# Reordering one layer's attention stage: half a gate ahead of an up projection, an earlier start of NSA attention, and another order of building operands

## The chip, the cores and the metric

The kernel runs on one core of a Trainium2 chip. The metric is the device time of one execution in microseconds (us); smaller is better. Five engines run side by side, each with its own queue worked off in order: PE (TensorE, matrix products), DVE (VectorE), ACT (ScalarE), POOL (GpSimd) and SP (which only issues transfers here). An instruction that waits holds up all that is queued behind it on its engine.

## The reference

One decoder layer on 256 tokens with a model width of 2048, in float32:

```python
xn = _rms(x, norm_attn[l])
(fq, fk, fv, f_logit, nq, kc, vc, ksl, vsl, kw, vw,
 nsa_gate, gate_a, gate_b) = jnp.split(xn @ w_in[l], points, axis=-1)
...
o_a = _fox_attention(fq, fk, fv, log_f)
...
merged = (jax.nn.sigmoid(gate_a) * (o_a @ w_up_fox[l])
          + jax.nn.sigmoid(gate_b) * (o_b @ w_up_nsa[l]))
x = x + (merged @ w_out[l]).astype(x.dtype)
hn = _rms(x, norm_ffn[l])
x = x + ((jax.nn.silu(hn @ w_ffn_gate[l]) * (hn @ w_ffn_up[l])) @ w_ffn_down[l]).astype(x.dtype)
```

FoX attention has 8 heads of 128 with a forget decay. NSA attention has 8 heads of 192 in two groups, and each head adds three softmaxes (compressed, selected, window), each with its own gate. The 2048 columns of `sigmoid(gate_a)` multiply the FoX up projection column by column.

## The kernel before

Every float32 matrix is split into a rounded part `hi` and a rest `lo`, and a product is made of three matmuls: hi·hi, hi·lo, lo·hi. ACT makes `hi` of a weight tile (L171), DVE makes `lo` (L172). The tokens stand in two tiles of 128 rows (`t` = 0, 1).

The program is one long list, `stream`, which a loop at the end walks. Its first part, up to the index `ffn`, consists of *chunks*: 256 rows of a weight, 512 columns at most, 12 matmuls (L194 to L196) into the two `acc` banks of a projection (four banks in all, so that two projections can hold banks at once). The chunks are the input projection, then `w_up_fox`, then two projections of 512 columns each for the first half of `gate_a` (`ga_chunk`). A chunk's weights are loaded up to 8 chunks ahead and split up to 3 ahead (`SPLIT_AHEAD`).

From `ffn` on come *pairs*: 256 rows and 1024 columns of a weight. A plain pair has 24 matmuls. A *seven* has 21: it works on sums of operand blocks in the way of Strassen, and its weights are split in two parts. The first unit of eight pairs makes the second half of `gate_a`. A pair's 1 MB of raw weights is loaded by SP (L1092) into three tiles in turn, the third of which lies in the pool `ypool`; its `hi`, `lo` lie in one of four part buffers. A *thin* pair takes half of its `lo` by a DMA that adds the weights onto −hi (L1114, L1115).

Beside the stream run *tasks*, Python generators: after every chunk one slot, after every pair two slots, and in a slot up to two tasks emit their next step. `yield n` means that the next step comes n slots later. This sets where a task's instructions stand in each engine's queue. The tasks that matter here:

- `head_norm` and its callers make the normed queries and keys out of `acc` banks; the NSA queries come in four tasks (`st["nq"]`), one for each two heads. The last read of the banks is L354, L356.
- `fox_attention`: 10 steps. Step s makes the output of head s−2, the transposes of head s−1 (L711), the scores of head s (L722, L723) and its softmax (`softmax_parts`: DVE maximum L678, ACT exponential L680). `divide` (L683 to L689) is the DVE work that ends a softmax; the transposes need it.
- `nsa_attention`: the same for 10 steps, with transposes L774 to L780, scores L801 to L805, outputs L760 to L764. It first waits, slot by slot, until the tasks that it needs and the FoX task are over.
- `x_seven`: makes the operand of a seven for two k blocks of x (seven blocks of 128 columns, 7·128·2 floats a partition), four steps: DVE L1237, ACT L1238; DVE L1241, L1244, L1245 and ACT L1243; ACT L1247; DVE L1249. `x_sevens` makes the four in turn, begun nine chunks before `ffn`.

`up_a_evac` copies the FoX up projection to the tiles `ga` (L893 on ACT, L894 on DVE); `ga_chunk` later makes the sigmoid into a scratch tile (L908 on ACT) and multiplies it on (L910 on DVE).

Of the kernel before, what the change touches and what calls it, by code (L numbers as in the profile page):

```python
# [14 lines left out]
P = 128  # L15
# [39 lines left out]
def hybrid_block(ctx: ExitStack, tc: tile.TileContext, x, norm_attn, w_in, fox_f_bias,  # L55
# [80 lines left out]
    def spawn(gen):  # L136
        tk = Task(gen)
        tasks.append(tk)
        return tk
# [556 lines left out]
    def fox_attention():  # L696
# [3 lines left out]
        for s in range(FH + 2):  # L700
# [14 lines left out]
            if h < FH:  # L715
# [10 lines left out]
                                        (sc[:, 0:P], bf[:, 0:P], pb[h][:, 0:P])], None)  # L726
                yield 1
                divide()
                yield 2
            else:  # L730
                yield 3


    def nsa_attention():
        for tk in st["nq"][:1] + [st["gate"], st["cmp", 0], st["cmp", 1], st["fox"]]:
            while not tk.over:
                yield 1
        qa, qb = st["nqa"], st["nqb"]
# [9 lines left out]
        for s in range(NH + 2):  # L748
            if 0 < s <= NH:
                divide()  # L750
            h = s - 2
            if h >= 0:
# [35 lines left out]
            if h < NH:  # L788
# [7 lines left out]
                for c0, n, t in ((0, 272, 1), (272, 256, 1), (P, 272, 0)):  # L796
# [16 lines left out]
                                        (sc[0][:, 256:271], bf[:, 527:542], p[:, 784:799])], gsw[:, h])  # L813
            yield 1 if 5 < s else 2

# [16 lines left out]
    def nq_evac(h0, c0):  # L832
        def done(accs):
            if "nqa" not in st:
                st["nqa"] = u8(ypool, [P, NH, T])
                st["nqb"] = u8(ypool, [P, NH, T], F32R)
            if c0:
                st["decay"] = spawn(fox_decay([accs[t][:, 0:8] for t in range(NT)]))
            st.setdefault("nq", []).append(spawn(nsa_qk(
                accs, c0, 2, DK ** -0.5, lambda t, a, b: put_q(h0, a, b, t))))  # L840
            if h0 == 2:
                st["nsa"] = spawn(nsa_attention())
        return done
# [3 lines left out]
    def proj(c0, n, done, **kw):  # L847
        return gemm(w_in, c0, n, KB, sx, done, **kw)
# [38 lines left out]

    def up_a_evac(i):
        def done(accs):
            if i == 0:  # L890
                ga.extend(u8(mpool, [P, D]) for _ in range(NT))
            sl = slice(i * 512, (i + 1) * 512)
            nc.scalar.activation(ga[0][:, sl], accs[0], AF.Copy)  # L893
            nc.vector.tensor_copy(ga[1][:, sl], accs[1])  # L894
        return done
# [4 lines left out]
    for i in range(4):  # L900
        stream += gemm(w_up_fox, i * 512, 512, 8, stat_o("oTf"), up_a_evac(i))


    def ga_chunk(i):
        def done(accs):
            for t in range(NT):
                g = wk([P, 512], "qs", 4)
                nc.scalar.activation(g, accs[t], AF.Sigmoid, scale=rx[:, t:t + 1])  # L908
                sl = ga[t][:, i * 512:(i + 1) * 512]
                nc.vector.tensor_tensor(sl, sl, g, op=ALU.mult)  # L910
        return done

    for i in range(2):
        stream += proj(OFF_GA + 512 * i, 512, ga_chunk(i))

# [315 lines left out]
    def x_seven(kp, pool):  # L1231
# [13 lines left out]
        nc.vector.tensor_tensor(fo[:, 3], ao[:, 2], fo[:, 2], op=ALU.add)  # L1245
        yield 1
        nc.scalar.activation(d[:, 0, 3:7].rearrange("p o t -> p (o t)"), f, AF.Copy)  # L1247
# [8 lines left out]
    def x_sevens():  # L1256
        for kp in range(4):
            yield from x_seven(kp, ypool if kp < 3 else xpool)
            yield 1

    def put_m(kp, where):
# [6 lines left out]
    SX = (0, 1, 2, 3)  # L1268
    unit((4, 5, 0, 6, 1, 3, 2, 7), SX[:3], two(w_in, 0, OFF_GA + 1024), x_pair(SX[:3]), ga_evac(1), thin=(6, 7))
    for i in range(2):  # L1270
# [136 lines left out]
    def run_att(i, ch):  # L1407
        nonlocal nload
        if i == ffn - 9:
            open2()  # L1410
            spawn(x_sevens())
        while nload < min(i + LOAD_AHEAD, ffn):
# [114 lines left out]
```

## Time and profile before

| | |
|---|---|
| time, median of 3 runs | 1429.4 us (1429.39 to 1431.14) |
| the profiled execution's own time | 1432.12 us |
| its span, first to last instruction | 1430.4 us |
| PE busy | 1413.9 us, 99% of the span |
| DVE, ACT, POOL busy | 1189.7, 845.5, 119.0 us |
| granted TensorE clock, mean | 0.997 of full |

PE is the engine that all others serve. Its busy time counts a matmul from start to a modelled end, and matmuls overlap; so the time between two starts, not a matmul's own length, tells how fast PE goes: some 0.23 us for 512 columns and 0.17 us for 384. A row of a timeline that ends in brackets tells that the engine was idle before it, for how long, and what ended the wait. The clock that PE is granted has two levels, 1.2 and 2.4 GHz, shown as 0.5 and 1.0 of full.

### The profile page before, as it was taken

What the parts mean: (1) busy time and instruction counts of PE and PEld (TensorE: products, weight loads), DVE (VectorE), ACT (ScalarE), POOL (GpSimd) and SP (SyncE); (2) the same over time, 40 slices, a digit from 0 to 9 for tenths busy, and PEclk for the clock granted to TensorE, in tenths of its full rate; (3) what the DMA queues carried; (4) which work ended last, traced back from release to release, by engine and by line L of the source; (5) the groups of instructions that cost most, each with busy time, mean ns of one, the idle gap of its engine ahead of it and who ended that gap; (6) DMA issues with size and microseconds to landing.
All of it is one profiled execution on the core that took longest, in us unless ns stands there. A gap on an engine that the chain in (4) does not pass through costs nothing.

```text
span 1430.4 us, 18345 instructions
## 1 busy us (share of the span) xinstructions
PE 1413.9 (99%) x6692; PEld 1188.3 (83%) x6692; DVE 1189.7 (83%) x1536; ACT 845.5 (59%) x1075; POOL 119.0 (8%) x123
## 2 busy tenths in 40 slices
PE   9999999999999999999999999999999999999998
PEld 7888888998888878888888888888888888888887
DVE  6676866776776798779898999988999988899985
ACT  5566554456665566465566667556667645666742
POOL 0211010000000010010020001011101000110000
PEclk9999999999999999999999999999999999999999
DMA  7667876454346588786786787679888677988785
GB/s 273 199 220 209 258 244 181 132 154 137 119 136 202 162 242 265 227 235 173 255 239 206 222 271 214 234 219 251 246 238 243 222 212 235 247 247 241 219 240 159
DMA packets 167350, 308.58 MB, mean 216 GB/s; under 512 B 10286, under 2 KB 33420, under 8 KB 167132
## 3 DMA queue, kind: packets, MB, share of 16 engines
q1 hardware_dynamic: 150396, 273.77, 58.4%
q0 software_dynamic: 16688, 33.37, 13.5%
q8 instruction: 52, 0.85, 0.2%
q14 instruction: 38, 0.31, 0.1%
q10 hardware_dynamic: 176, 0.27, 0.1%
HBM read 298.98 MB, written 8.40 MB: 215 GB/s over the span
## 4 chain that ended last, share of the span: by engine, by line
PE 88%; DVE 3%; issue 3%; DMA 3%; ACT 2%; POOL 0%; SPq 0%; POOLq 0%; DVEq 0%; ACTq 0%
PE m L1144 15%; PE m L1145 14%; PE m L1143 14%; PE acc L194 8%; PE acc L196 8%; PE acc L195 8%; PE acc L1143 5%; PE acc L1145 5%; PE acc L1144 5%; DMA lo<-in_w_ffn_up_dram 1%; DVE lo L172 1%; PE acc L1060 1%; PE m L559 1%; PE m L560 1%; ACT hi L171 1%
## 5 line engine op out<-in xcount | busy, mean ns | idle before, releaser
L1121 DVE TENSOR_TENSOR lo<-raw,hi 128x2048 fp32r<-128x2048 f32 (+2 forms) x168 | 305.9, 1823 | 33.9 <-ACT hi L1119 16.9
L1119 ACT ACTIVATE hi<-raw 128x1536 fp32r<-128x1536 f32 (+1 forms) x129 | 217.3, 1687 | 107.3 <-PE m L1145 53.6
L172 DVE TENSOR_TENSOR lo<-raw,hi 128x1024 fp32r<-128x1024 f32 (+5 forms) x165 | 189.4, 1152 | 92.9 <-ACT hi L171 88.3
L1112 ACT ACTIVATE hi<-sums 128x1024 fp32r<-128x1024 f32 x148 | 154.5, 1059 | 140.2 <-PE m L1145 63.9
L194 PE MATMUL acc<-hi,u 128*128 128x512 f32 (+4 forms) x576 | 223.2, 388 | 2.5 <-ACT u L893 1.2
L196 PE MATMUL acc<-hi,u 128*128 128x512 f32 (+4 forms) x576 | 217.7, 378 | 0.0
L195 PE MATMUL acc<-lo,u 128*128 128x512 f32 (+4 forms) x576 | 217.4, 377 | 0.0
L171 ACT ACTIVATE hi<-raw 128x1024 fp32r<-128x1024 f32 (+5 forms) x165 | 161.9, 1001 | 68.6 <-PE acc L196 49.7
L1121 DVE TENSOR_TENSOR lo<-sums,hi 128x2048 fp32r<-128x2048 f32 x74 | 169.1, 2285 | 7.3 <-ACT hi L1112 7.0
L1144 PE MATMUL m<-lo,u 128*128 128x512 f32 x352 | 137.4, 390 | 2.1 <-DVE lo L1121 1.7
L1144 PE MATMUL m<-lo,hp 128*128 128x512 f32 x352 | 137.2, 390 | 1.4 <-DMA lo<-in_w_ffn_up_dram 1.4
L1143 PE MATMUL m<-hi,hp 128*128 128x512 f32 x352 | 137.9, 392 | 0.0
L1143 PE MATMUL m<-hi,u 128*128 128x512 f32 x352 | 137.4, 390 | 0.0
L1145 PE MATMUL m<-hi,hp 128*128 128x512 f32 x352 | 137.1, 389 | 0.0
L1145 PE MATMUL m<-hi,u 128*128 128x512 f32 x352 | 137.0, 389 | 0.0
L194 PEld LDWEIGHTS acc<-hi,u 128*128 128x128 f32 x576 | 108.9, 189 | 19.5 <-ACT u L893 1.7
L196 PEld LDWEIGHTS acc<-hi,u 128*128 128x128 f32 x576 | 108.7, 189 | 17.7 <-DVE u L277 0.7
L195 PEld LDWEIGHTS acc<-lo,u 128*128 128x128 f32 x576 | 108.9, 189 | 15.0
L1102 DVE TENSOR_TENSOR sums<-raw 128x1024 f32<-128x1024 f32 x68 | 82.9, 1219 | 1.0 <-DMA raw<-in_w_ffn_down_dram 0.7
L1144 PEld LDWEIGHTS m<-lo,u 128*128 128x128 f32 x352 | 66.1, 188 | 17.1 <-DVE lo L1121 2.3
L1144 PEld LDWEIGHTS m<-lo,hp 128*128 128x128 f32 x352 | 66.1, 188 | 15.7 <-DMA lo<-in_w_ffn_up_dram 2.4
L1145 PEld LDWEIGHTS m<-hi,hp 128*128 128x128 f32 x352 | 66.1, 188 | 13.7
(334 smaller groups left out, 2649.4 us busy)
## 6 DMA issues: line engine op xcount, KB each, us to landing
raw<-in_w_in_dram SPq DMA_DIRECT2D x111, 512.0 KB
raw<-in_w_ffn_gate_dram SPq DMA_DIRECT2D x88, 512.0 KB
raw<-in_w_ffn_up_dram SPq DMA_DIRECT2D x88, 512.0 KB
raw<-in_w_ffn_down_dram SPq DMA_DIRECT2D x88, 512.0 KB
lo<-in_w_ffn_up_dram POOLq DMA_DIRECT2D x30, 512.0 KB, 8.2
raw<-in_w_out_dram SPq DMA_DIRECT2D x28, 512.0 KB
raw<-in_w_in_dram SPq DMA_DIRECT2D x24, 384.0 KB
raw<-in_w_up_fox_dram SPq DMA_DIRECT2D x16, 512.0 KB
```

What stands on the lines that cost most here:

```text
L171: nc.scalar.activation(hi[:, :m], ch.raw[:, :m], AF.Copy)
L172: nc.vector.tensor_tensor(lo[:, :m], ch.raw[:, :m], hi[:, :m].bitcast(F32), op=ALU.subtract)
L194: nc.tensor.matmul(o, h, ch.hi[:, j], start=first and j == 0, stop=False)
L195: nc.tensor.matmul(o, h, ch.lo[:, j], start=False, stop=False)
L196: nc.tensor.matmul(o, l, ch.hi[:, j], start=False, stop=last and j == w - 1)
L1102: nc.vector.tensor_tensor(s[:, 0:2], w[:, 0].unsqueeze(1).to_broadcast([P, 2, 512]), w[:, 1:4:2], op=ALU.add)
L1112: nc.scalar.activation(hi[:, o:o + 2], src[:, o:o + 2], AF.Copy)
L1119: nc.scalar.activation(h, src, AF.Copy)
L1121: return lambda: nc.vector.tensor_tensor(l, src, h.bitcast(F32), op=ALU.subtract)
L1143: nc.tensor.matmul(o, h, hi, start=n == 0, stop=False)
L1144: nc.tensor.matmul(o, h, lo, start=False, stop=False)
L1145: nc.tensor.matmul(o, l, hi, start=False, stop=n + 1 == total[key])
```

## The change

Five edits. FoX `divide` follows its softmax at once, in the same step. The last FoX step starts the NSA task, which so stands some chunks earlier; in the NSA task one slot is put between the first `divide` and the first transposes, and one slot is added after step 3. The two gate projections move from behind the FoX up projection to ahead of it: their sigmoid now goes straight into `ga`, and the up projection's evacuation multiplies onto it (columns 0 to 1023) or copies as before (the rest). The x operands 0 and 1 are made side by side, then 3, all ahead of `ffn`, and 2 behind it; operand 3 replaces operand 2 in the first unit, so that each unit has as many sevens as before. The count of PE instructions is the same.

```diff
@@ fox_attention
                                         (sc[:, 0:P], bf[:, 0:P], pb[h][:, 0:P])], None)
-                yield 1
                 divide()
-                yield 2
-            else:
+            if s < FH + 1:
                 yield 3
+        st["nsa"] = spawn(nsa_attention())
@@ nsa_attention
-        for tk in st["nq"][:1] + [st["gate"], st["cmp", 0], st["cmp", 1], st["fox"]]:
-            while not tk.over:
-                yield 1
+        for tk in st["nq"][:1] + [st["gate"], st["cmp", 0], st["cmp", 1]]:
+            finish(tk)
...
             if 0 < s <= NH:
                 divide()
+                if s == 1:
+                    yield 1
...
-            yield 1 if 5 < s else 2
+            yield 1 if 5 < s else 3 if s == 3 else 2
@@ nq_evac
-            if h0 == 2:
-                st["nsa"] = spawn(nsa_attention())
@@
+    def ga_chunk(i):
+        def done(accs):
+            if i == 0:
+                ga.extend(u8(mpool, [P, D]) for _ in range(NT))
+            for t in range(NT):
+                nc.scalar.activation(ga[t][:, i * 512:(i + 1) * 512], accs[t], AF.Sigmoid, scale=rx[:, t:t + 1])
+        return done
+
+    for i in range(2):
+        stream += proj(OFF_GA + 512 * i, 512, ga_chunk(i))
+
     def up_a_evac(i):
         def done(accs):
-            if i == 0:
-                ga.extend(u8(mpool, [P, D]) for _ in range(NT))
-            sl = slice(i * 512, (i + 1) * 512)
-            nc.scalar.activation(ga[0][:, sl], accs[0], AF.Copy)
-            nc.vector.tensor_copy(ga[1][:, sl], accs[1])
+            o = [g[:, i * 512:(i + 1) * 512] for g in ga]
+            if i < 2:
+                for t in range(NT):
+                    nc.vector.tensor_tensor(o[t], accs[t], o[t], op=ALU.mult)
+            else:
+                nc.scalar.activation(o[0], accs[0], AF.Copy)
+                nc.vector.tensor_copy(o[1], accs[1])
         return done
...
-    def ga_chunk(i):
-        def done(accs):
-            for t in range(NT):
-                g = wk([P, 512], "qs", 4)
-                nc.scalar.activation(g, accs[t], AF.Sigmoid, scale=rx[:, t:t + 1])
-                sl = ga[t][:, i * 512:(i + 1) * 512]
-                nc.vector.tensor_tensor(sl, sl, g, op=ALU.mult)
-        return done
-
-    for i in range(2):
-        stream += proj(OFF_GA + 512 * i, 512, ga_chunk(i))
@@ x_seven
         nc.vector.tensor_tensor(fo[:, 3], ao[:, 2], fo[:, 2], op=ALU.add)
-        yield 1
+        yield 2
@@ x_sevens
-        for kp in range(4):
-            yield from x_seven(kp, ypool if kp < 3 else xpool)
+        yield from x_seven(1, ypool)
+        yield 1
+        yield from x_seven(3, xpool)
+        while here[0] < ffn:
             yield 1
+        yield from x_seven(2, ypool)
@@
-    unit((4, 5, 0, 6, 1, 3, 2, 7), SX[:3], two(w_in, 0, OFF_GA + 1024), x_pair(SX[:3]), ga_evac(1), thin=(6, 7))
+    unit((4, 5, 0, 6, 1, 2, 3, 7), (0, 1, 3), two(w_in, 0, OFF_GA + 1024), x_pair((0, 1, 3)), ga_evac(1),
+         thin=(6, 7))
@@ run_att
             open2()
+            spawn(x_seven(0, ypool))
             spawn(x_sevens())
```

Three places in the instruction order, before and after. Line numbers of the changed kernel are lower by two at the places shown (its L1235 is L1237 of before, its L1100 is L1102), and its L891 is the sigmoid of a gate.

On DVE, the softmax of FoX head 6 and what follows it (`p` are its exponentials, `lo` the rest of a weight chunk, `u` the output of an earlier head). Before:

```order
L678 ISA p_635_2957,mx_2958<-m_2954,bias_2951 128x128
L678 ISA mx_2958 128x1
L172 TENSOR_TENSOR lo_2970<-raw_2815,hi_2969 128x768
L683 TENSOR_SCALAR mx_2959<-mx_2959 128x2
L685 RECIPROCAL mx_2986<-mx_2959 128x2
L689 TENSOR_SCALAR p_635_2957<-p_635_2957,mx_2986 128x256
L689 TENSOR_SCALAR p_635_2957<-p_635_2957,mx_2986 128x128
```

And now:

```order
L678 ISA p_637_2960,mx_2961<-m_2957,bias_2954 128x128
L678 ISA mx_2961 128x1
L683 TENSOR_SCALAR mx_2962<-mx_2962 128x2
L685 RECIPROCAL mx_2968<-mx_2962 128x2
L689 TENSOR_SCALAR p_637_2960<-p_637_2960,mx_2968 128x256
L689 TENSOR_SCALAR p_637_2960<-p_637_2960,mx_2968 128x128
L172 TENSOR_TENSOR lo_2977<-raw_2815,hi_2976 128x768
```

The four rows of `divide` moved ahead of the split of a weight chunk; they now stand directly behind the maximum, whose exponentials ACT has still to make.

On ACT, the evacuation of the first gate projection. Before, beside two heads of NSA (`L893` is a copy of the up projection):

```order
L171 ACTIVATE hi_3862<-raw_3681 128x1024
L893 ACTIVATE u_830_3878<-acc_3710 128x512
L171 ACTIVATE hi_3888<-raw_3704 128x1024
L693 ACTIVATE u_714_3311<-m_3916 128x256
L171 ACTIVATE hi_3937<-raw_3752 128x1024
```

And now, at the same head's output (`L693`):

```order
L171 ACTIVATE hi_4027<-raw_3864 128x1024
L891 ACT_TABLE_LOAD
L891 ACTIVATE u_862_4043<-acc_3750,rx 128x512
L891 ACTIVATE u_863_4044<-acc_3751,rx 128x512
L693 ACTIVATE u_700_3244<-m_4057 128x256
L171 ACTIVATE hi_4073<-raw_3906 128x1024
...
L793 ACTIVATE bias_4138<-base 128x542
L680 ACT_TABLE_LOAD
L680 ACTIVATE p_885_4158,mx_4160<-p_885_4158,mx_4159 128x256 x2
```

Sigmoids now stand between exponentials, and each change of the function brings a table load: seven in the whole program where there were three.

On DVE, the first unit of pairs, from the sums of its second seven (`sums`) on. `F` are the scratch tiles of an x operand. Before:

```order
L1237 TENSOR_TENSOR F_4935<-u_7_120 128x512
L1102 TENSOR_TENSOR sums_4942<-raw_1009_4849 128x1024
L1104 TENSOR_TENSOR sums_4942<-sums_4942,raw_1009_4849 128x512
...
L1241 TENSOR_TENSOR F_4936<-F_4935 128x256
L1244 SCALAR_TENSOR_TENSOR F_4936<-F_4936,F_4935 128x128
L1245 TENSOR_TENSOR F_4936<-F_4935,F_4936 128x128
L1121 TENSOR_TENSOR lo_5000<-u_1013_4860,hi_4999 128x2048
```

And now:

```order
L1235 TENSOR_TENSOR F_4894<-u_7_120 128x512
L1239 TENSOR_TENSOR F_4895<-F_4894 128x256
L1242 SCALAR_TENSOR_TENSOR F_4895<-F_4895,F_4894 128x128
L1243 TENSOR_TENSOR F_4895<-F_4894,F_4895 128x128
...
L1100 TENSOR_TENSOR sums_4939<-raw_1005_4846 128x1024
L1102 TENSOR_TENSOR sums_4939<-sums_4939,raw_1005_4846 128x512
```

The last x operand stood around the split of this seven; now it is worked off ahead of it, and between this seven and the next pair nothing of x is left but its last step.

## Rows read from the trace of the kernel before

**Rows 1.** The page, busy time of an engine, its share of the span, and its instructions.

```profile
PE 1413.9 (99%) x6692; PEld 1188.3 (83%) x6692; DVE 1189.7 (83%) x1536; ACT 845.5 (59%) x1075; POOL 119.0 (8%) x123
```

**Rows 2.** The view that gives each engine's busy time by stretch, over all stretches of 10 us; shown are the four lowest of the twelve in which PE is busy for less than its 10 us. The columns are: stretch, its length, busy us (instructions) of PE, PEld, DVE, ACT, POOL, granted clock as a share of full, DMA share, GB/s.

```profile
290.00:300.00 10.00, 8.22 (x50) 7.96 (x49) 7.26 (x19) 4.97 (x14) 1.24 (x1) 1.00 0.47 125
...
330.00:340.00 10.00, 7.08 (x42) 6.64 (x42) 6.15 (x17) 4.41 (x10) 0.00 (x0) 0.83 0.34 108
...
370.00:380.00 10.00, 8.23 (x34) 6.29 (x33) 5.34 (x14) 3.96 (x11) 1.98 (x1) 0.83 0.40 127
...
500.00:510.00 10.00, 8.32 (x37) 6.81 (x37) 9.92 (x9) 6.89 (x6) 1.22 (x1) 1.00 0.57 171
```

**Rows 3.** Timelines of PE, ACT and DVE at FoX head 6. The columns are: start us, duration us, engine, line, operation, output<-inputs, shape, count, and in brackets the idle time before it and what ended it.

```profile
294.38 0.19 ACT L680 ACTIVATION_READ_ACCUMULATOR p<-p,mx 128x1 f32 x1
...
293.61 0.08 DVE L678 DVE_READ_ACCUMULATOR2_ANT mx<- 128x1 f32 x1
295.73 0.96 DVE L172 TENSOR_TENSOR lo<-raw,hi 128x768 fp32r<-128x768 f32 x1 [2.04 <-ACT hi L171]
...
297.00 0.55 DVE L689 TENSOR_SCALAR p<-p,mx 128x256 f32<-128x256 f32 x2
...
297.70 0.52 PE L711 MATMUL m<-ident,p 128*128 128x128 f32 x3 [1.78 <-DVE p L689]
```

**Rows 4.** Timelines of PE and DVE at the start of NSA attention: the end of the scores of head 0, the transposes of head 0, the fourth matmul behind them; the same eight transposes for head 1 at 348.30 and the matmul behind them; and on DVE the end of the maximum, a norm with a split behind it, and the divide.

```profile
326.05 0.29 PE L805 MATMUL m<-kbl,u 128*128 128x272 f32 x1
...
333.86 1.11 PE L774 MATMUL m<-ident,p 128*128 128x128 f32 x4 [2.92 <-DVE p L689]
...
336.58 0.41 PE L194 MATMUL acc<-hi,u 128*128 128x384 f32 x1
...
348.30 0.60 PE L774 MATMUL m<-ident,p 128*128 128x128 f32 x4
...
349.09 0.42 PE L194 MATMUL acc<-hi,u 128*128 128x384 f32 x1
...
321.20 0.23 DVE L350 TENSOR_SCALAR sm<-sm,rx 128x2 f32<-128x2 f32 x1 [0.90 <-POOL sm L297]
...
322.13 0.95 DVE L172 TENSOR_TENSOR lo<-raw,hi 128x768 fp32r<-128x768 f32 x1
...
326.99 0.08 DVE L678 DVE_READ_ACCUMULATOR2_ANT mx<- 128x1 f32 x1
...
332.99 1.29 DVE L689 TENSOR_SCALAR p<-p,mx 128x256 f32<-128x256 f32 x6
```

**Rows 5.** The view by stretch, for PE alone, behind the two longest waits. The columns are: stretch, length, PE busy (matmuls), granted clock, DMA share, GB/s.

```profile
334.00:337.00 3.00, 3.00 (x13) 0.54 0.24 93
...
374.00:376.00 2.00, 1.70 (x4) 0.57 0.58 173
```

**Rows 6.** Timelines of PE and DVE at the start of the second up projection (PE), and the norm of the last two NSA queries (DVE).

```profile
372.80 0.50 PE L194 MATMUL acc<-hi,u 128*128 128x512 f32 x1 [1.24 <-ACT u L893]
...
374.30 0.80 PE L194 MATMUL acc<-hi,u 128*128 128x512 f32 x1 [0.54 <-DVE u L894]
...
378.03 0.28 PE L760 MATMUL m<-pt,vhl 128*128 128x256 f32 x1
...
380.75 0.56 DVE L354 TENSOR_TENSOR qs<-acc,sm 128x384 f32<-128x384 f32 x1
```

**Rows 7.** Timelines of PE, ACT and DVE in the first unit of pairs: its first matmul, its two waits, and what stood ahead of the split that PE waited for.

```profile
473.88 0.39 PE L1143 MATMUL m<-hi,u 128*128 128x512 f32 x1
...
501.78 0.50 PE L1144 MATMUL m<-lo,u 128*128 128x512 f32 x1 [1.68 <-DVE lo L1121]
...
515.31 0.50 PE L1144 MATMUL m<-lo,u 128*128 128x512 f32 x1 [0.29 <-DMA lo<-in_w_in_dram]
...
496.96 0.63 ACT L1247 ACTIVATE u<-F 128x512 fp32r<-128x512 f32 x1 [3.27 <-DVE F L1245]
497.50 1.90 ACT L1119 ACTIVATE hi<-u 128x2048 fp32r<-128x2048 f32 x1
```

**Rows 8.** Timeline of ACT: the wait ahead of the exponentials of two NSA heads, and a table load with the sigmoids behind it.

```profile
340.76 0.51 ACT L680 ACTIVATE p<-p,mx 128x256 f32<-128x256 f32 x1 [0.50 <-DVE mx L678]
...
368.15 0.51 ACT L680 ACTIVATE p<-p,mx 128x256 f32<-128x256 f32 x1 [1.21 <-DVE mx L678]
...
450.72 1.28 ACT L908 ACT_TABLE_LOAD   x1
452.02 1.26 ACT L908 ACTIVATE qs<-acc,rx 128x512 f32<-128x512 f32 x2
```

**Rows 9.** For the first unit: two pieces of the chain of waits (start us, us, what), the transfers of the third pair on SP's timeline, the split of the third pair on DVE (two sums, then `lo` of its first and second part), and from the view by stretch two microseconds in which the transfers were densest (columns as in rows 2).

```profile
502.16 4.90 DMA u<-in_w_in_dram
...
507.26 8.00 DMA lo<-in_w_in_dram
...
454.79 0.98 SPq L1092 DMA_DIRECT2D u<-in_w_in_dram  x2
...
476.07 1.22 DVE L1102 TENSOR_TENSOR sums<-u 128x1024 f32<-128x1024 f32 x1
...
478.66 1.75 DVE L1121 TENSOR_TENSOR lo<-u,hi 128x1536 fp32r<-128x1536 f32 x1
480.32 2.29 DVE L1121 TENSOR_TENSOR lo<-sums,hi 128x2048 fp32r<-128x2048 f32 x1
...
456.00:458.00 2.00, 2.00 (x10) 1.66 (x9) 1.85 (x4) 0.93 (x3) 0.00 (x0) 1.00 1.06 406
```

More of the change, by code (lines that the diff above doesn't have):

```diff
@@ L886, in hybrid_block @@
     ga = []
-    def up_a_evac(i):
+    def ga_chunk(i):
         def done(accs):
@@ L891, in done, with up_a_evac @@
                 ga.extend(u8(mpool, [P, D]) for _ in range(NT))
-            sl = slice(i * 512, (i + 1) * 512)
-            nc.scalar.activation(ga[0][:, sl], accs[0], AF.Copy)
-            nc.vector.tensor_copy(ga[1][:, sl], accs[1])
+            for t in range(NT):
[3 more added lines that the diff above has]
+        stream += proj(OFF_GA + 512 * i, 512, ga_chunk(i))
+    def up_a_evac(i):
+        def done(accs):
[6 more added lines that the diff above has]
+                nc.vector.tensor_copy(o[1], accs[1])
         return done
```

## The prediction

> **What bounds the kernel now.** I read the page first: PE is busy for 99% of the span [rows 1], so the time is PE's, and the only thing an edit of the order can win is a stretch in which PE waits or runs at the lower clock. The view by stretches of 10 us then shows where: of 143 stretches PE falls short in twelve, and the four largest lie at 290, 330, 370 and 500 us [rows 2], just where this change works. In the timelines of PE I looked for the bracket in each of the four.
>
> - A, FoX head 6: PE waits 1.78 us before its transposes for DVE's `divide` [rows 3]. ACT had the exponentials ready at 294.57 (294.38 + 0.19), but DVE first took a `lo` that itself waited for `hi`, to 296.69, and ended the divide at 297.55.
> - B, NSA head 0: PE waits 2.92 us for the first `divide` [rows 4], because in the first step the transposes stand right behind it in one slot.
> - C, second up projection: PE waits 1.24 and 0.54 us for the copies of the first one [rows 6]. DVE reads the last NSA queries' banks only at 380.75, so the two projections had to share two banks.
> - D, first unit of pairs: 1.68 us for a `lo`, and 0.29 us for a thin pair's transfer [rows 7]. ACT made that `hi` late since ahead of it stood L1247 of an x operand, which waited 3.27 us for DVE.
>
> Behind B and C the granted clock is 0.54 and 0.57, the lower of its two levels [rows 5]. The cost is read from starts. Behind B, eight transposes and three matmuls of 384 columns took 336.58 − 333.86 = 2.72 us; at the full clock the same transposes took 349.09 − 348.30 = 0.79 [rows 4] and three matmuls take 3 × 0.17, in all 1.31. So 1.4 us. Behind C, nine matmuls of 512 columns took 378.03 − 374.30 = 3.73 us [rows 6] in place of 9 × 0.23 = 2.05, so 1.7 us. Behind A and D no clock was lost (1.00 in both stretches, [rows 2]).
>
> So A is worth 1.78, B 4.3, C 3.5 and D 1.97: 11.5 us of 1430, the ceiling of this change.
>
> **Part by part.**
>
> *FoX divide at once.* Nothing is added; the four DVE rows move ahead of a `lo`. At head 6 the divide can start when ACT's exponentials end, 294.6, and takes 0.9 (296.69 to 297.55), so it ends near 295.5; PE comes to the transposes at 297.70 − 1.78 = 295.92. A goes, with 0.4 us to spare. The price is that DVE now stands still for the exponentials at each of the eight heads, 293.69 to 294.57 at head 6, some 0.9 us; behind it stand the `lo` of chunks that PE takes two or three chunks (12 matmuls, 2 us or more each) later. At head 6 DVE waited there anyway, 2.04 us for `hi` [rows 3]. I count nothing; if that cover is gone at every head, 8 × 0.9 = 7 us of DVE, of which PE sees what exceeds the lead. I take 1.7 for A.
>
> *NSA begun earlier, with a slot behind the first divide.* Between the scores of head 0 and its transposes PE now has 36 matmuls of 384 columns, 36 × 0.17 = 6.2 us (24 before). DVE has in this time, from the end of the scores (326.05 + 0.29): 0.73 to the end of the maximum (326.99 + 0.08); then two norms with a `lo` each, which the order puts there now, (322.13 + 0.95 − 321.20) = 1.9 us each; then the divide, 0.6 of small rows and 1.29 [rows 4]: 0.7 + 3.8 + 1.9 = 6.4 us. That is a tie. The wait shrinks from 2.92 to between 0 and about 1 us, too short for a clock loss if A's 1.78 caused none. I take 3.7 of 4.3. Later heads keep their distances.
>
> *Gate projections ahead of the up projection.* The first gate projection is 8 chunks long in place of 4, some 22 us at 0.23 × 96, and the queries' norm ends inside it, so the second finds free banks: on DVE it stands behind the maximum of NSA head 4, whose scores PE makes 24 matmuls (5.5 us) and an output ahead of the second gate's start, against a maximum of under 0.8 us and a norm of 1.9 on DVE [rows 4]. C goes: 3.4. Two copies on each of ACT and DVE and four multiplies become two copies and four multiplies; ACT and DVE are not the bound, so nothing is counted for it. The new cost is four table loads, since sigmoids now stand between NSA's exponentials. A load took 1.28 us on ACT [rows 8], so 4 × 1.28 = 5.1 us of ACT. The loads for the exponentials stand just where ACT waits for DVE's maximum, 0.50 and 1.21 us at two heads [rows 8], those for the sigmoids where ACT waits for PE's last matmuls of the projection. Left over is at most 1.28 − 0.50 = 0.8 us at two heads, on a chain that has a chunk of slack. Bounds: nothing to 5 us; I take 0.5, near the rows.
>
> The Trainium skill speaks against this edit: "ScalarE: Activation LUTs", section "Table sets: the hidden batching unit", says to do all work of one table set before switching, and its section "What ACT_TABLE_LOAD costs" puts a switch at 2.66 us, a drain included. By that, an estimate, four switches would be 10.6 us of ACT in place of 5.1. The row here shows the load at 1.28 us with the next sigmoid 0.02 us behind it, so the trace does not show the drain as a cost of its own.
>
> *x operands.* Operand 3 no longer stands in the first unit, and 2 stands early in it, so L1247 is not in front of the fifth pair's `hi` late in the unit: both waits of D can go. But the third pair's raw tile (1 MB, in `ypool`) now takes the place of FoX's output, which the up projection reads to its last matmul. Before, that transfer was issued at 454.79, 19 us ahead of the unit [rows 9]; now it can only be issued when the unit begins. From there: about 1 us to issue (0.98), 4.90 to land, two sums and half a third, 478.66 − 476.07 = 2.6, `lo` 1.7 and 2.2 [rows 9]. The first part is ready 1.0 + 4.9 + 2.6 + 1.7 = 10.2 us and the second 12.4 us behind the start of the unit. PE needs them after 48 matmuls, 48 × 0.23 = 11.0 us, and after nine more, 13.1 us. It just fits. The fourth pair is thin: its transfer starts behind this and took 8.00 us in this unit [rows 9] at worst; it may be 1 to 2 us late. I take 1.2 of the 1.97.
>
> **The sum.** 1.7 + 3.7 + 3.4 + 1.2 − 0.5 = 9.5 us. The profiled execution took 1432.1 (its span 1430.4), so 1422.6 for it; it is 2.7 above the median of the runs. On the median of 1429.4 the forecast is 1419.9, that is 0.66% faster. Behind 520 us PE is busy but for some 5 us far away, and its work does not change, so the shift goes through to the end.
>
> **The rivals.**
>
> 1. *B only moves.* DVE's tie is lost, PE waits for the first divide as long as before and drops its clock. For it: 6.4 against 6.2 us. Against it: a wait of a few tenths is not 2.92. Then 3.7 falls away: 1423.6.
> 2. *The burst at the unit's start.* The loads of pairs 3 to 6 now all become free together, 4 MB, and share the DMA engines. If they land together rather than in turn, 4 MB at the 400 GB/s that the engines moved at 456 us [rows 9] take 10.5 us, and with the issue the third pair lands 11.5 behind the start; its first `lo` is there 2.6 + 1.7 later, at 15.8. PE, which needs it at 11.0, waits 4.8 us and loses some 1.5 of clock, as behind B. D gives nothing and 6.3 are lost: 1429.4 − (1.7 + 3.7 + 3.4 − 0.5) + 6.3 = 1427.4. For it: four transfers where two stood. Against it: the third pair's are issued first.
> 3. *Slower: NSA's heads 1 to 4.* They now lie beside the norms of two query pairs and both sigmoids. If DVE and ACT fall behind, each head's transposes wait as head 0's did, 2.92 + 1.4 = 4.3 us. It decides from three heads on: four cost 17, and 1429.4 − 9.5 + 17 = 1437. For it: DVE works its queue off in order, and each edit puts more ahead of a divide. Against it: head 1 went without a wait before [rows 4], with a distance that is the same now, and DVE was busy for only 6.15 and 5.34 of 10 us in these stretches [rows 2].
> 4. *Nothing but the FoX edit works*: B as in rival 1, the second gate's banks as late as C's were, D as before: 1429.4 − 1.7 = 1427.7.
>
> **How the numbers follow.** Forecast 0.68, rival 1 0.13, rival 2 0.08, rival 3 0.06, rival 4 0.05. The forecast's own range is the ceiling, 1429.4 − 11.5 = 1417.9, less 1 for what the rows do not show (small waits in A to D that I left out), to 1422.5. The range takes in rival 1 with a margin and reaches towards rivals 2 and 4: 1416.8 to 1427.0; left out are rivals 2 to 4, 0.19. Within 0.2%, about what a measurement of this kernel can tell from no change, is 1426.5 to 1432.3. Faster: the forecast, rival 1 and a little of rival 2, 0.82; same: the rest of 2, and rival 4, 0.12; slower: rival 3, 0.06.
>
> **What would show it.** In the profile after: no wait of PE at FoX transposes; at most 1 us ahead of the first NSA transposes and a clock of 1.0 there; no wait at the first matmul of any up projection; in the first unit of pairs, waits at the third or fourth pair of under 2 us in all, and none at the sixth. A granted clock under 0.9 in any stretch of 10 us between 280 and 520 would prove the sum wrong, as would a PE idle sum there above 4 us.

## The result, and the profile after

The changed kernel took 1421.45 us (median of six runs, 1419.94 to 1423.40) against 1430.79 for the kernel before beside it (six runs): a ratio of 0.9935, 95% interval 0.9923 to 0.9948, or 9.3 us less. The forecast was 1419.9 with a range of 1416.8 to 1427.0. The profiled execution took 1423.4 us, its span 1421.7, 8.7 less than the span before. The four places fared as follows (us of PE time, read from the timelines of PE):

| place | before | after | forecast gain | gain |
|---|---|---|---|---|
| A, FoX head 6 (and an accumulator at 307) | 1.78 + 0.38 | 0 + 0.29 | 1.7 | 1.9 |
| B, first NSA heads | 2.92 + 1.4 of clock | 1.55 + 0.18 | 3.7 | 2.6 |
| C, second projection behind NSA's queries | 1.24 + 0.54 + 1.7 of clock | 0 | 3.4 | 3.5 |
| D, first unit of pairs | 1.68 + 0.29 | 0 | 1.2 | 2.0 |
| table loads | | nothing on PE | −0.5 | 0 |

Added up before rounding that is 9.9 us where 9.5 were forecast. Two of the terms are off by about 1 us each, B down and D up, and that they nearly cancel is luck. In the view by stretches of 10 us, the four stretches of [rows 2] are whole again, but B's wait now lies in the stretch before; between 280 and 520 us PE falls short by more than 0.02 us only here (columns as in [rows 2]):

```profile
300.00:310.00 10.00, 9.71 (x57) 9.18 (x57) 8.84 (x30) 4.96 (x12) 0.00 (x0) 1.00 0.53 157
...
320.00:330.00 10.00, 8.45 (x53) 8.13 (x52) 7.75 (x30) 5.41 (x18) 0.00 (x0) 1.00 0.37 110
...
340.00:350.00 10.00, 9.82 (x64) 9.30 (x63) 7.52 (x30) 6.56 (x20) 1.01 (x1) 1.00 0.62 179
```

The granted clock is 1.00 in all of them. What is left is mostly B. The timelines of PE and DVE there, which answer to [rows 4], read:

```profile
328.09 0.63 PE L774 MATMUL m<-ident,p 128*128 128x128 f32 x4 [1.55 <-DVE p L689]
...
320.94 0.08 DVE L678 DVE_READ_ACCUMULATOR2_ANT mx<- 128x1 f32 x1
322.90 0.96 DVE L172 TENSOR_TENSOR lo<-raw,hi 128x768 fp32r<-128x768 f32 x1 [1.88 <-ACT hi L171]
...
326.51 0.16 DVE L683 TENSOR_SCALAR mx<-mx 128x6 f32<-128x6 f32 x1
...
327.13 1.29 DVE L689 TENSOR_SCALAR p<-p,mx 128x256 f32<-128x256 f32 x6
```

From the end of the maximum (321.02) DVE stood 1.88 us for a `hi`, then worked off two norms with a `lo` each (322.90 to 326.51), then the divide (to 328.42; PE began at 328.09, behind its first part).

The rest of the program adds noise of its own size. In the profiled run of the changed kernel the first matmuls of the first weight chunk stand 0.43 us apart (timelines of PE, the third and fourth of them, the changed kernel):

```profile
8.16 0.63 PE L196 MATMUL acc<-hi,u 128*128 128x512 f32 x1
8.59 0.63 PE L194 MATMUL acc<-hi,u 128*128 128x512 f32 x1
```

and in the kernel before 0.29, and 0.23 from there on:

```profile
7.09 0.45 PE L196 MATMUL acc<-hi,u 128*128 128x512 f32 x1
7.38 0.40 PE L194 MATMUL acc<-hi,u 128*128 128x512 f32 x1
```

PE reaches its thirtieth `hi`·`lo` triple at 30.65 us in place of 28.33, so 2.3 us were lost there, in code that the change does not touch. From that point to the last matmul the changed kernel is 11.0 us shorter. The four places give 9.9 of it, and 0.6 are two waits for transfers of the feed-forward weights behind 800 us, which are there in both kernels (0.60 and 0.82 before, 0.61 and 0.23 after). One other profile of the study, that of the run with the gates undone, shows the same start (its thirtieth triple at 30.3); in the other twelve, the kernel before's among them, that point lies between 28.1 and 28.9.

### The profile page after: what moved, and what is told of

It is laid out like the page before. It is cut to its first block, busy times and chain, and to the rows that moved or that the text cites. A ratio compares the mean times of both kernels' runs of the same rounds, so it can differ in the third digit from the quotient of the medians.

```text
span 1421.7 us, 18346 instructions
## 1 busy us (share of the span) xinstructions
PE 1412.7 (99%) x6692; PEld 1187.4 (84%) x6692; DVE 1189.1 (84%) x1534; ACT 850.6 (60%) x1077; POOL 117.5 (8%) x123
## 4 chain that ended last, share of the span: by engine, by line
PE 93%; DVE 2%; issue 2%; DMA 1%; ACT 1%; POOL 0%; ACTq 0%; POOLq 0%; DVEq 0%
PE m L1142 15%; PE m L1141 15%; PE m L1143 15%; PE acc L194 8%; PE acc L196 8%; PE acc L195 8%; PE acc L1141 6%; PE acc L1142 5%; PE acc L1143 5%; PE acc L1058 1%; DMA lo<-in_w_ffn_up_dram 1%; PE m L559 1%; PE m L560 1%; DMA lo<-in_w_ffn_down_dram 0%; DVE lo L172 0%
## 5 line engine op out<-in xcount | busy, mean ns | idle before, releaser
L1100 DVE TENSOR_TENSOR sums<-raw 128x1024 f32<-128x1024 f32 x68 | 83.0, 1221 | 1.6 <-DMA raw<-in_w_ffn_down_dram 1.3
L1143 PEld LDWEIGHTS m<-hi,u 128*128 128x128 f32 x352 | 66.1, 188 | 13.7
```

What stands on the lines that cost most here:

```text
L1100: nc.vector.tensor_tensor(s[:, 0:2], w[:, 0].unsqueeze(1).to_broadcast([P, 2, 512]), w[:, 1:4:2], op=ALU.add)
L1143: nc.tensor.matmul(o, l, hi, start=False, stop=n + 1 == total[key])
```

## The experiments

Twelve kernels were run, each against the kernel before on the same chip. Five timed runs or more stand behind every ratio; the 95% intervals are about 0.0012 to either side, 1.8 us, so two such kernels are told apart by the ratio only from some 2.5 us on, and for less the waits of PE in the trace decide.

| run | ratio (95%) | waits of PE between 280 and 520 us |
|---|---|---|
| the change | 0.9935 (0.9923 to 0.9948) | 0.29, 1.55, 0.18 |
| FoX divide undone | 0.9948 (0.9936 to 0.9961) | 1.78, 0.38, 0.68, 0.97 |
| no slot | 0.9957 (0.9944 to 0.9969) | 0.31, 3.62 and clock, 0.29, 0.96 |
| gates undone | 0.9928 (0.9916 to 0.9941) | 0.30, 1.54, 0.16 |
| x undone | 0.9976 (0.9967 to 0.9985) | 0.31, 1.54, 0.16, then 3.73 and clock |
| gates and x undone | 0.9949 (0.9937 to 0.9962) | 0.29, 1.54, 0.16, 1.68, 0.57 |
| NSA late | 0.9939 (0.9927 to 0.9952) | 0.30, 2.92 |
| NSA late, gates undone | 0.9963 (0.9950 to 0.9977) | 0.30, 2.92, 1.24, 0.53 and clock |

**The FoX divide undone.**

```diff
+                yield 1
                 divide()
-            if s < FH + 1:
+                yield 2
+            elif s < FH + 1:
                 yield 3
```

> The changed kernel with the FoX divide a chunk behind its softmax again. Theory (each wait belongs to its own edit): PE waits some 1.8 us for DVE's divide at one FoX head, as in [rows 3], and nowhere else anew; ratio to the kernel before 0.9948, against 0.9935 of the changed kernel. Rival (the wait at that head came from the queries' norms beside it and is gone since NSA stands elsewhere): no wait at any FoX head, ratio 0.9935.

Ratio 0.9948. The wait is back to the hundredth (timeline of PE):

```profile
298.04 0.52 PE L711 MATMUL m<-ident,p 128*128 128x128 f32 x3 [1.78 <-DVE p L689]
```

So A is the divide's place in DVE's queue. The edit is not wholly apart from B, though: with these other `yield`s the scores of the first NSA head also stand two chunks later in PE's queue (24 matmuls of the stream). There the first head waits 0.68 us in place of 1.55, and the seventh 0.97 (timeline of PE):

```profile
332.18 0.66 PE L776 MATMUL m<-ident,p 128*128 128x128 f32 x4 [0.68 <-DVE p L689]
```

**The slot behind the first NSA divide taken out.**

```diff
-                if s == 1:
-                    yield 1
```

> The changed kernel without the slot between the first NSA divide and its transposes: PE comes to the transposes 12 matmuls (2.07 us) earlier, DVE's queue up to the divide is the same. Theory (the divide is set by DVE's queue, not by PE): the divide ends at the same moment, the wait grows from 1.55 to 3.6 us, and the clock falls behind it as in [rows 5], 1.4 more: 3.5 us slower than the changed kernel, ratio 0.996. Rival (the earlier start of NSA alone removes the wait): 1.5 us or less of wait, ratio 0.9935.

Ratio 0.9957, 3.1 us behind the change. The wait grew by 12 matmuls, from 1.55 to 3.62, and the clock fell (timeline of PE, then the view by stretch, columns as in [rows 2]):

```profile
326.24 1.09 PE L772 MATMUL m<-ident,p 128*128 128x128 f32 x4 [3.62 <-DVE p L689]
...
320.00:330.00 10.00, 6.38 (x32) 5.96 (x31) 7.01 (x21) 3.68 (x9) 0.00 (x0) 0.83 0.28 79
```

So the moment of the divide is set by DVE's queue, and the slot only gives PE something to do until then.

**The gates behind the up projection again.** The stream, `ga_chunk` and `up_a_evac` as before, all else as changed:

```diff
-    for i in range(2):
-        stream += proj(OFF_GA + 512 * i, 512, ga_chunk(i))
     for i in range(4):
         stream += gemm(w_up_fox, i * 512, 512, 8, stat_o("oTf"), up_a_evac(i))
+    for i in range(2):
+        stream += proj(OFF_GA + 512 * i, 512, ga_chunk(i))
```

> The changed kernel with the two gate projections behind the FoX up projection again (and three table loads). Theory (the banks of the last NSA queries are held past 377 us): the second up projection waits 1.2 and 0.5 us for the copies and runs its first matmuls at the lower clock, 3.5 us slower than the changed kernel, ratio 0.996. Rival (the earlier NSA start brings the norm forward far enough): no wait, ratio 0.9935 or, if the four table loads cost something, lower by up to 0.5 us, 0.993.

The theory fell: ratio 0.9928, no wait at the second up projection. Its timelines (ACT and DVE: the copies of the first up projection; PE: the first NSA output behind that projection, then the first matmul of the second):

```profile
369.28 0.63 ACT L891 ACTIVATE u<-acc 128x512 f32<-128x512 f32 x1
...
370.87 0.69 DVE L892 COPY u<-acc 128x512 f32<-128x512 f32 x1
...
369.81 0.28 PE L760 MATMUL m<-pt,vhl 128*128 128x256 f32 x1
...
371.24 0.48 PE L194 MATMUL acc<-hi,u 128*128 128x512 f32 x1
```

Here too DVE reads the NSA queries' last bank only at 381.12, so the two up projections share two banks as before. But the 13 matmuls of an NSA output (1.4 us) now stand between them, and ACT is not busy with a head's exponentials. In the kernel before, ACT worked off six exponentials, two small copies and a `hi` first, and began to copy 0.6 us behind the end of PE's last matmul of the projection:

```profile
371.18 0.39 PE L196 MATMUL acc<-hi,u 128*128 128x512 f32 x1
...
371.22 1.05 ACT L171 ACTIVATE hi<-raw 128x1024 fp32r<-128x1024 f32 x1
372.16 0.58 ACT L893 ACTIVATE u<-acc 128x512 f32<-128x512 f32 x1
```

**The x operands undone**, first alone, then with the gates:

```diff
-        yield from x_seven(1, ypool)
-        yield 1
-        yield from x_seven(3, xpool)
-        while here[0] < ffn:
-            yield 1
-        yield from x_seven(2, ypool)
+        for kp in range(4):
+            yield from x_seven(kp, ypool if kp < 3 else xpool)
+            yield 1
...
-    unit((4, 5, 0, 6, 1, 2, 3, 7), (0, 1, 3), ...
+    unit((4, 5, 0, 6, 1, 3, 2, 7), SX[:3], ...
```

> The changed kernel with the x operands made in turn as before, and the first unit's order of pairs and operands as before. Theory (ACT's copy of an x operand delays a hi in the unit): PE waits 1.5 to 2 us for a lo at the fifth pair and 0.3 for a thin pair, ratio 0.9948. Rival (those waits hung on NSA's last heads, which now end earlier): no wait, ratio 0.9935.

> Both the gates and the x operands as before; FoX divide at once and the earlier NSA start stay. Theory (the x edit repairs what the gates ahead bring, the late third raw tile and a full DVE at the unit's start): the waits in the first unit are those of [rows 7], 2.0 us in all and not the 3.7 and a fall of the clock that the run with x alone undone showed; ratio 0.9943. Rival (the x edit is worth 5 us by itself): 5 us slower than the run with the gates alone undone, ratio 0.9963.

Ratios 0.9976 and 0.9949. With the gates ahead, the old order of the operands costs 5.9 us on the change, not 2 (timeline of PE, then a stretch of 2 us behind the last wait):

```profile
483.52 0.50 PE L1141 MATMUL m<-hi,u 128*128 128x512 f32 x1 [0.69 <-ACT hi L1115]
484.79 0.50 PE L1142 MATMUL m<-lo,u 128*128 128x512 f32 x1 [0.76 <-DVE lo L1119]
495.90 0.50 PE L1141 MATMUL m<-hi,u 128*128 128x512 f32 x1 [0.46 <-ACT hi L1117]
498.23 0.50 PE L1142 MATMUL m<-lo,u 128*128 128x512 f32 x1 [1.82 <-DVE lo L1119]
...
500.00:502.00 2.00, 2.00 (x6) 1.52 (x6) 1.97 (x3) 1.66 (x2) 0.00 (x0) 0.50 1.01 380
```

With the gates behind it is the 1.68 of [rows 7] and 0.57 for a thin pair:

```profile
494.15 0.50 PE L1142 MATMUL m<-lo,u 128*128 128x512 f32 x1 [1.68 <-DVE lo L1119]
...
507.94 0.50 PE L1142 MATMUL m<-lo,u 128*128 128x512 f32 x1 [0.57 <-DMA lo<-in_w_in_dram]
```

So the theory held: the x edit pays for a cost that the gates ahead bring, besides D itself. The place is the third pair's raw tile. With the gates behind, its transfer is issued at 446.92; with them ahead at 467.23, the unit's first matmul being at 467.03. DVE, which makes its sums first, stands 4.00 us for it, and the steps of an x operand that still have to follow push the next `hi` of ACT back: its copy L1245 stands ahead of that `hi` and waits 3.28 us for DVE. It does so with the gates behind too, but there it starts 9.8 us behind the unit's first matmul, and here 13.1 (timelines of SP with the gates behind, then of SP, DVE and ACT with them ahead):

```profile
446.92 1.18 SPq L1090 DMA_DIRECT2D u<-in_w_in_dram  x2
...
467.23 0.88 SPq L1090 DMA_DIRECT2D u<-in_w_in_dram  x2
...
472.52 1.23 DVE L1100 TENSOR_TENSOR sums<-u 128x1024 f32<-128x1024 f32 x1 [4.00 <-DMA u<-in_w_in_dram]
...
480.09 0.63 ACT L1245 ACTIVATE u<-qs 128x512 fp32r<-128x512 f32 x1 [3.28 <-DVE qs L1243]
```

In the changed kernel DVE stands for the tile as long (4.31 us, shown further down), but there the first three operands are all but made.

**NSA's start.** A first attempt put back the code that polls for the end of the FoX task, without the slot and without the added slot behind step 3:

> The changed kernel with the start of NSA attention as before (behind the FoX task, no slot behind the first divide, no added slot behind step 3); gates stay ahead, FoX divide at once, x operands new. Theory of the prediction (gates ahead alone remove C, because the second gate finds free banks): only the wait for the first NSA divide is back, 2.9 us with 1.4 of clock, no wait at the start of any gate or up projection; 2.7 us slower than the changed kernel, ratio 0.9954. Rival (C went because NSA's heads fall elsewhere against the end of a projection): a wait of about 1 us and a fall of the clock at a start of one of the projections as well, ratio 0.997 to 0.998.

Ratio 0.9955 (0.9942 to 0.9967), with 3.62 us of wait as in the run without the slot: the edit missed its aim. What starts NSA three chunks earlier is that the last FoX step no longer ends with `yield 3`; the polling alone starts it at the same place (PE has 1212 matmuls of the stream ahead of the first scores in both). So that line went back as well:

```diff
-            if s < FH + 1:
-                yield 3
+            yield 3
-        st["nsa"] = spawn(nsa_attention())
```

> As the run with NSA's start as before, and the last FoX step again ends three slots later, so that NSA's first scores stand in PE's queue where they stood before (the run before this one had left them at the earlier place). Theory of the prediction (gates ahead alone remove C): the wait for the first divide is back with 2.9 us and 1.4 of clock, no wait at the start of a gate or up projection; 2.6 us slower than the changed kernel, ratio 0.9953. Rival (C went only because NSA's heads fall elsewhere): 1.2 and 0.5 us of wait and a fall of the clock at a projection's start too, ratio 0.998.

Ratio 0.9939, where 0.9953 was expected: the wait of 2.92 us is back, but in the profiled run the clock did not fall behind it (see the last section). No projection waits. The second gate's first matmul stands at 383.33, while ACT reads the first gate's banks only at 384.97, and DVE had left the queries' banks at 378.76: it runs in free banks (timelines of PE and ACT, and of DVE):

```profile
331.87 0.66 PE L771 MATMUL m<-ident,p 128*128 128x128 f32 x4 [2.92 <-DVE p L689]
...
383.33 0.39 PE L194 MATMUL acc<-hi,u 128*128 128x512 f32 x1
...
384.97 1.27 ACT L890 ACTIVATE u<-acc,rx 128x512 f32<-128x512 f32 x2
...
378.48 0.28 DVE L356 TENSOR_TENSOR qs<-acc,sm 128x128 f32<-128x128 f32 x1
```

**Both the gates and NSA's start as before**, with the FoX divide and the x operands alone left in:

> Gates and NSA's start both as before: only the FoX divide at once and the x operands stay. Theory (either of the two edits takes C away, neither of the others does): the wait for the first divide of 2.9 us and, at the second up projection, waits of 1.2 and 0.5 us as in [rows 6], with or without a fall of the clock behind each (up to 1.4 and 1.7); A and D stay away; 1.8 + 2.0 us faster than the kernel before, ratio 0.9973. Rival (C was a matter of 1.8 us of phase and went with the FoX edit alone): no wait at the second up projection, ratio 0.995.

Ratio 0.9963. Without either edit C is back (timeline of PE, and the stretch behind it):

```profile
369.68 0.50 PE L194 MATMUL acc<-hi,u 128*128 128x512 f32 x1 [1.24 <-ACT u L890]
371.18 0.61 PE L194 MATMUL acc<-hi,u 128*128 128x512 f32 x1 [0.53 <-DVE u L891]
...
372.00:374.00 2.00, 2.00 (x6) 1.60 (x5) 1.90 (x10) 0.00 (x0) 1.26 (x1) 0.50 0.76 244
```

**The first divide earlier.** One chunk earlier on DVE, the transposes left where they are, with the gates ahead and with the gates behind; then at once, as in FoX, with the gates behind:

```diff
                 if s == 1:
-                    yield 1
+                    yield 2
...
-            yield 1 if 5 < s else 3 if s == 3 else 2
+            yield 1 if 5 < s or s == 0 else 3 if s == 3 else 2
```

> The changed kernel with the first NSA divide emitted one chunk earlier, its transposes where they are. Theory (the divide was late since DVE first stood for a hi behind ACT's six exponentials and then worked off two norms): the divide ends at 326.3, PE comes at 326.5, no wait, 1.55 us faster than the changed kernel, ratio 0.9924. Rival (the divide moves but something behind it, the norm or a lo, is late in its place): a wait of 1 us or more within the next three chunks, ratio 0.9935.

> The same early divide with the gates as before: only the FoX edit, the NSA edits and the x operands stay. Theory (the gates ahead give nothing): no wait of over 0.4 us between 280 and 520 us, as fast as the same with gates ahead or faster, ratio 0.992. Rival (gates ahead save what was hidden by the later waits): 1 us or more slower than it.

> Gates as before, and the first NSA divide directly behind its softmax on DVE, as in FoX; transposes where they are. Theory (DVE stands 1.9 us for a hi there anyway, so the 1.6 us of the divide fit into it and the norms come only 0.8 us later): no wait at the first transposes, none or under 0.2 us for the second norm in place of the 0.53 of the run with the divide one chunk earlier; 0.7 us faster than that run, ratio 0.9926. Rival (the norms are late all the same): 0.5 us of wait at the accumulators again.

Ratios 0.9935 (0.9921 to 0.9948), 0.9931 (0.9919 to 0.9944) and 0.9927 (0.9913 to 0.9940). One chunk earlier, the wait at the transposes is gone in both, but the second norm behind the divide is late in its place, 0.52 us, and the next head 0.42; at once, only the latter is left (timelines of PE, the first of these runs):

```profile
325.88 0.44 PE L194 MATMUL acc<-hi,u 128*128 128x384 f32 x1 [0.52 <-DVE qs L356]
...
339.26 0.66 PE L774 MATMUL m<-ident,p 128*128 128x128 f32 x4 [0.42 <-DVE p L689]
```

and the last (PE, then DVE):

```profile
338.71 0.66 PE L774 MATMUL m<-ident,p 128*128 128x128 f32 x4 [0.41 <-DVE p L689]
...
319.78 0.17 DVE L683 TENSOR_SCALAR mx<-mx 128x6 f32<-128x6 f32 x1 [1.14 <-ACT p L680]
...
321.61 0.95 DVE L172 TENSOR_TENSOR lo<-raw,hi 128x768 fp32r<-128x768 f32 x1
```

That shows the missed term of B: DVE stands there for 1.88 us, and the divide, put first, uses part of it. DVE waits 1.14 us for the exponentials, and the `lo` starts 2.97 us behind the maximum's end (318.64) in place of 1.88. So 0.8 of the divide's 1.9 us cost nothing, and the second norm is no longer late. The last of the three, without the gates' move, has the least waiting of all kernels here, 0.71 us between 280 and 520 where the change has 2.02. Its five runs took 1419.55 to 1420.49 us, median 1419.95; that is 10.9 below the kernel before, but against the changed kernel the ratios overlap, so only the trace says that it is faster, by about 1.3 us.

**Ten more table loads.** A sigmoid of one column was added behind the softmax of six heads; its result is used by nothing.

```diff
+                if h < 6:
+                    nc.scalar.activation(wk([P, 1], "tl", 1), rx[:, 0:1], AF.Sigmoid)
```

> The changed kernel with a sigmoid of one column behind the softmax of each of NSA's heads 0 to 5, whose result is used by nothing: 17 table loads in place of 7. Theory (a load costs ACT 1.28 us, and one fits where ACT waits for DVE or PE): ten loads are 13 us of ACT, at most 0.5 us of new waits of PE for each head that has them ahead of its first chunks, 0 to 3 us in all, ratio 0.9935 to 0.9956. Rival (a load drains the engine, 2.66 us a switch by the Trainium skill, "ScalarE: Activation LUTs", "What ACT_TABLE_LOAD costs"): 27 us of ACT, heads late by more than their chunk of slack, 6 us or more, ratio 0.998.

Ratio 0.9981 (0.9973 to 0.9990): 6.6 us slower than the change, twice the most that the theory allowed and what the rival named. The waits are 3.04, 1.52 and 2.00 at three heads, 6.56 where the change has 1.73, and the clock fell behind the first. But the mechanism is not the rival's. A load takes 1.28 us and the next function starts 0.02 behind it (timeline of ACT):

```profile
319.72 0.19 ACT L680 ACTIVATION_READ_ACCUMULATOR p<-p,mx 128x1 f32 x1
319.91 1.28 ACT L815 ACT_TABLE_LOAD   x1
321.21 0.20 ACT L815 ACTIVATE tl<-rx 128x1 f32<-128x1 f32 x1
321.31 2.30 ACT L171 ACTIVATE hi<-raw 128x768 fp32r<-128x768 f32 x3
```

The load stands ahead of the `hi` for which DVE stands at B, so that it adds itself, with its 0.2 of sigmoid, to the 1.55 of wait; at heads 1 and 2 a second load stands ahead of the exponentials besides. The Trainium skill ("ScalarE: Activation LUTs", "What ACT_TABLE_LOAD costs") counts a drain of 1.38 us with each load. The trace shows none on either side of this one: the read ahead of it ends where the load starts, and the sigmoid follows at once, so that here a switch costs ACT 1.30 us.

## Why the prediction came out

Right by its own steps: PE is the bound, and the gain is the sum of the waits at four places; no clock under 0.9 is left, and PE's waits between 280 and 520 us sum to 2.02, under the 4 that was named as what would prove the sum wrong.

Of the signs that it named, one failed: "at most 1 us ahead of the first NSA transposes" was 1.55. One reading was off without harm: two other stretches of 10 us are as low as the four named (PE busy 8.22 us at 0 and 6.04 at 1420), the program's start and end.

*A* (1.7 forecast) was 1.78, and undoing the edit brought back 1.78. The price that was counted as nothing, DVE standing for the exponentials at each head, did not reach PE: from 9 us to the 0.29 at 307 PE waits nowhere in the changed kernel.

*B* (3.7 forecast, 2.6 measured) was mis-sized. The step that failed is "0.7 + 3.8 + 1.9 = 6.4 us. That is a tie". The maximum, the norms and the divide took what was said or a little less (0.73, 3.6, and 1.6 until PE could start). Left out was DVE's 1.88 us of standing for ACT's `hi`, which sits behind the head's six exponentials. The trace had the row for it: the kernel before shows the same wait there, in the timeline of DVE:

```profile
328.94 0.96 DVE L172 TENSOR_TENSOR lo<-raw,hi 128x768 fp32r<-128x768 f32 x1 [1.88 <-ACT hi L171]
```

A sum of DVE's busy times along its queue is no forecast of when the queue gets somewhere; the waits inside it count. That the clock stays up behind such a wait was right (1.00 behind 1.55 us).

*C* (3.4 forecast, 3.5 measured) came out in size, and its reason holds but is not the only one. "The queries' norm ends inside it, so the second finds free banks" is shown by the run with NSA late, beside the one with neither edit. Overlooked was that the earlier start of NSA removes C by itself, by putting an output's matmuls and a free ACT at the projection's end (so the timelines show it; the two were not tried apart). Each of the two edits is enough; with neither, C is back. So the gates' move, with its four table loads and the x edit's burden, earned nothing that can be measured in this kernel: without it the ratio is 0.9928 and the waits are the same.

*D* (1.2 forecast, 2.0 measured) was mis-sized to the cautious side. The burst that was feared fits, a little better than worked out (timelines of PE, SP and DVE in the changed kernel: first matmul of the unit, the third pair's transfer, its sums and its two `lo`):

```profile
468.82 0.39 PE L1141 MATMUL m<-hi,u 128*128 128x512 f32 x1
...
468.79 0.88 SPq L1090 DMA_DIRECT2D u<-in_w_in_dram  x2
...
474.02 1.23 DVE L1100 TENSOR_TENSOR sums<-u 128x1024 f32<-128x1024 f32 x1 [4.31 <-DMA u<-in_w_in_dram]
...
476.62 1.75 DVE L1119 TENSOR_TENSOR lo<-u,hi 128x1536 fp32r<-128x1536 f32 x1
478.29 2.29 DVE L1119 TENSOR_TENSOR lo<-sums,hi 128x2048 fp32r<-128x2048 f32 x1
```

The parts are ready 9.6 and 11.8 us behind the unit's start; 10.2 and 12.4 were forecast, 11.0 and 13.1 needed. So rival 2 did not come: the transfers behind it did not hold back the first. What the forecast did not see is that the x edit is needed for this, since the old order costs 5.9 us with the late tile, against 3.0 with the gates behind (0.9949 against 0.9928).

*Table loads* (0.5 forecast) cost nothing on PE: the run without the four has the same waits. The loads stand where ACT has slack; that is a matter of place, as ten more in a worse place showed.

Rival 1 (B only moves) was partly true, with 1.55 of 2.92 us left and no fall of the clock. Rival 3 (slower, NSA's heads fall behind) did not happen; the run with more loads shows that its mechanism exists, when ACT's queue is held at three heads. Rival 4 (the FoX edit alone works) did not come either; no run has that edit alone, the nearest, with FoX and x, has 0.9963.

## What to carry to other kernels

When the time until an in-order engine gets to an instruction decides, add up its idle brackets as well as its work, and look for them in the kernel before: another engine's queue sets them, and they are also the place where moved work costs nothing. Where a change has several parts, undo each alone and two together: here one part (the gates) was covered by another and made a third necessary. For gains of less than the runs' interval, the waits in the trace tell what the times can't.

## What the runs showed of the hardware

The same wait does not always cost the clock. Ahead of the first NSA transposes PE waited 2.92 us in the kernel before and the clock was 0.54 behind it ([rows 5]); in the profiled executions of two kernels (NSA late, with gates ahead and behind) it waited the same 2.92 and the clock stayed at 1.00: in the row at 331.87 above the four transposes took 0.66 us, against 1.11 in [rows 4]. Behind 3.62 and 3.04 us it fell, behind 2.00 and 1.55 it didn't. And C's two waits, of 1.24 and 0.53 us with three matmuls between them, cost the clock in both kernels that have them. One kernel's executions differ too, by the mean granted clock on record for each. With NSA late it is 1.000 in the profiled one and 0.998 in two of the other four, where all six of the changed kernel read 1.000; without the slot, one of five reads 1.000, though the profiled one fell behind 3.62. So a price for the clock of 1.4 to 1.7 us is a chance and not a fixed sum, and these runs are too few for its odds.

The start of the program shows the lower speed without a sign in the column of the granted clock. In the changed kernel's profile the matmuls from 7.7 to 10.7 us stand 0.43 us apart, about as far as at the lower of the two levels behind C (nine in 3.73 us). The view by stretch says 1.00 and counts 6 matmuls in 2 us. But the clock records of this trace begin only at 11.1 us, and at 5.6 us in that of the kernel before, so this 1.00 stands for no record (the first row is the changed kernel's):

```profile
8.00:10.00 2.00, 2.00 (x6) 1.61 (x6) 1.73 (x3) 1.06 (x1) 0.00 (x0) 1.00 1.05 388
```

The kernel before, in the same stretch:

```profile
8.00:10.00 2.00, 2.00 (x13) 1.64 (x12) 1.31 (x2) 1.09 (x2) 0.00 (x0) 1.00 1.05 396
```

At 2.3 us this could make up most of the spread between runs of one kernel (1419.94 to 1423.40). Only the profiled runs can be looked into; the two that start so are the slowest of their kernels (1423.40 of six, 1422.55 of five). It is a quarter of what the change gained.
